# Last block of a three-layer model on one core: TensorE's order written by hand from the gates to the first out projection

## The chip, the core and the metric

The kernel runs on one core of a Trainium2 chip. A core has TensorE for matrix products (PE, with PEld for its weight loads), VectorE (DVE), ScalarE (ACT), GpSimd (POOL) and SyncE (SP), which here only starts transfers. The engines run beside each other, each through its own list of instructions in a fixed order, and wait for one another on semaphores. The metric is the time of one execution on the device in microseconds, the median over several runs.

## The reference, cut to what matters

Input is one sequence of 1024 tokens, 1024 wide, in 32-bit floats. Two layers of a first model come first (windowed attention beside a state-space mixer, then attention on selected keys). The change touches only the block behind them:

```
h    = layer_norm(x)
proj = h @ w_in                      # xs, z, bm, cm, dt, glu, cgate
xbc  = silu(causal_conv4(xs, bm, cm))
dt   = softplus(dt + dt_bias);  a_cs = cumsum(dt * a) in chunks of 128
y    = diagonal(cm, bm, a_cs, xs*dt) + off_diagonal(cm, state, a_cs) + d_skip*xs
y    = group_rms(y * silu(z)) * g
u    = glu[:1024] * sigmoid(glu[1024:])
u    = silu(layer_norm(causal_conv31(u))) * silu(cgate)
out  = concat(y, u) @ w_out + b_out
h    = layer_norm(ALPHA*h + out);  then a gated product and another layer norm
```

The scan over eight chunks carries a state per group (two groups of eight heads) from chunk to chunk. Both z and cgate ("the gates") are products of the normed input with parts of `w_in`.

## The kernel before, in words

All products are made in three passes of a split number: an operand is a rounded high part and the rest, and `mm3` (lines 149 to 151) adds high x high, high x low and low x high. A *product* here is one output tile of 128 x 512 over eight slices of 128 rows of the contraction: eight *steps* of three matmuls, 24 matmuls. The normed input lies transposed in one tile, `hnT`, for the whole block; weights are loaded in pieces of 128 x 512 by `wpiece` (SP starts the transfer, ScalarE or VectorE rounds, GpSimd or VectorE subtracts) into 13 rotating buffers, or into three more of the stage's own pool.

`phase_c` is the last block. In program order it makes: the GLU products, eight channel tiles of u; in `xbc` the products dt, bm, cm and xs with their short convolution (four taps, all on VectorE, lines 1544 and 1546); the long convolution of 31 taps on VectorE, one channel tile after the other, in two accumulation banks (1286 and 1288), and the sum over the channels in `acc` (1291); `conf_norm`, the layer norm over the channels: the mean by a matmul (1490), the subtraction on VectorE (1495), the squares on ScalarE (1497), their sum on GpSimd (1501), the variance by small matmuls (1505), its root on GpSimd, its spread over the rows by matmul (1510), the multiplication on VectorE (1515) and the silu on ScalarE (1516); `ssd`, first the step sizes (a softplus written out as a series, 1567 to 1611, whose running sums go to memory as `d_cs`), then the scan; the cgate products, 16 of them, stored to `d_cg`; the multiplication of the convolution's result by them (16 halves, GpSimd, 1313); the z products, 16 of them, stored to `d_z`; and the first half of the out projection (the lines from 1327 on), which reads the convolution's result split by ScalarE and GpSimd (`msC`, 1335 and 1336) and adds the residual and the bias.

In each chunk of the scan, per group: a tile of decays is loaded from `d_cs` (`ld`), shifted on VectorE (1629), made an exponential on ScalarE (1631) and multiplied by the product of cm and bm (1642); GpSimd scales the input to `xd`, `xe` and `xh` (1644 to 1647); TensorE makes `cb`, `yoff` from the state, `ydiag` from decay and `xd`, and `inc`, by which VectorE updates the state.

Who comes when is not the program's order. The framework orders each engine's instructions itself, by what it estimates to be ready, keeping what the data demand; only the marked `high_priority` and `issue_after` places push it. What it keeps is the order in which tiles of one tag take that tag's buffers: the program's order. TensorE has two banks for products (`mm`), three for the scan and the norm (`sd`), one for transposes and two for the long convolution. A pool that is closed hands its place to the next one, whose tiles wait until the old tile there is no longer read.

The block's second out projection follows, with its own layer norm, and then the gated product with the output.

Of the kernel before, what the change touches and what calls it, by code (L numbers as in the profile page):

```python
# [20 lines left out]
P = 128  # L21
L = 1024
# [35 lines left out]
class K:  # L58
# [94 lines left out]
    def form1(self, out, hnT, tok0, wt, nk, w, wc0=0, start=True, stop=True):  # L153

        for k in range(nk):
            self.mm3(out, hnT[:, 0, k, tok0:tok0 + P], hnT[:, 1, k, tok0:tok0 + P],
                     wt[k][:, 0, wc0:wc0 + w], wt[k][:, 1, wc0:wc0 + w],
                     start and k == 0, stop and k == nk - 1)

# [1078 lines left out]
def phase_c(k, out, hC):  # L1238
# [15 lines left out]
    def stage():  # L1254
        return stg.tile([P, 512], F32, tag="s", name="stg", bufs=3)
# [4 lines left out]
    sV, (up,) = stack(k.pool("c_u"))  # L1260
    for j in range(4):
# [14 lines left out]
    with ExitStack() as cx:  # L1276
        xbc(k, cx.enter_context(k.pool("c_xbc")), W, hnT, sw, dtt, d_xs, d_bc)

    acc = up.tile([P, L], F32, name="acc")
# [18 lines left out]
    for ch in range(2):  # L1298
        w = k.wchunk(W, 4624 + ch * 512, 512)
        for m in range(4):  # L1300
            for th in range(2):
                ps = k.mm()
                k.form2(ps, hnT, th * 512, w, KT, m * P)
                gt = stage()
                S.activation(gt, ps, AF.Silu)
                r0 = (ch * 4 + m) * P
                nc.scalar.dma_start(d_cg[r0:r0 + P, th * 512:th * 512 + 512], gt)
    for ct in range(8):
        for th in range(2):
            cs = slice(th * 512, th * 512 + 512)  # L1310
            cg = stg.tile([P, 512], F32, tag="cg", name="cgl", bufs=2)
            nc.sync.dma_start(cg, d_cg[ct * P:(ct + 1) * P, cs])
            G.tensor_tensor(cc[:, ct, cs], cc[:, ct, cs], cg, op=ALU.mult)
    for ch in range(2):
        w = k.wchunk(W, 1024 + ch * 512, 512)
        for tt in range(NT):
            ps = k.mm()
            k.form1(ps, hnT, tt * P, w, KT, 512)
            zt = stage()
            S.activation(zt, ps, AF.Silu)  # L1320
            nc.scalar.dma_start(d_z[tt * P:(tt + 1) * P, ch * 512:ch * 512 + 512], zt)
    sR.close()
    k.wdve = WDVE[4]

    with ExitStack() as co:
        op = co.enter_context(k.pool("c_o", side="right"))
        bo = op.tile([P, D], F32, name="bo")
        k.bcast_row(bo, ins["b_out_2"][0], D)
        w = [[k.wpiece(Wo, kk + 8, [(ch * 512, 512)], pool=op if ch * 8 + kk >= 13 else None, nx=3)
              for kk in range(8)] for ch in range(2)]  # L1330
        held = []
        for tt in range(NT):
# [6 lines left out]
            V.scalar_tensor_tensor(r, r, ALPHA, bo, op0=ALU.mult, op1=ALU.add)  # L1339
            held.append((tt, m, r))  # L1340
            if tt == NT - 2:
                continue
            for ch in range(2):
                cs = slice(ch * 512, ch * 512 + 512)
                for t_, m, r in held:
                    ps = k.mm()
                    k.form1(ps, m, 0, w[ch], 8, 512)
                    V.tensor_tensor(r[:, cs], ps, r[:, cs], op=ALU.add)
                    nc.sync.dma_start(d_r[t_ * P:(t_ + 1) * P, cs], r[:, cs])
            held = []  # L1350
    sS.close()
    sF.close()

# [4 lines left out]
    with ExitStack() as co:  # L1358
# [4 lines left out]
        k.bcast_row(bb, ins["ln1_b_2"][0], D)  # L1363
        w = [[k.wpiece(Wo, kk, [(ch * 512, 512)], scale=sng[:, kk:kk + 1], pool=op if ch * 8 + kk >= 13 else None, nx=3)
              for kk in range(8)] for ch in range(2)]

        def prep(tt):
# [19 lines left out]
            nc.sync.dma_start(r, d_r[ts_, :])  # L1387
            return m, r
# [19 lines left out]
        for tt in range(NT):  # L1408
            pt = op.tile([P, 256], F32, tag="pt", name="pt", bufs=2)
# [72 lines left out]
def conf_norm(k, p, cc, acc, cw):  # L1482
# [5 lines left out]
    for th in range(2):  # L1488
        ps = k.ps("sd", "mu")
        T.matmul(ps, on, acc[:, th * 512:th * 512 + 512], start=True, stop=True)  # L1490
        mu.append(ps)
    for ct in range(8):
# [11 lines left out]
    for tt in range(NT):  # L1504
        T.matmul(ps[:, tt * 2:tt * 2 + 2], acc[:, tt * P:(tt + 1) * P], on[:, 0:2], start=True, stop=True)
# [194 lines left out]
```

## Time and profile before

| | us |
|---|---|
| median of three timed runs (2117.3 to 2118.9) | 2117.71 |
| the profiled execution | 2112.16 |
| its span, first to last instruction | 2110.3 |
| TensorE busy (9291 matmuls) | 1931.6, 92% |
| VectorE busy | 1513.9, 72% |
| ScalarE busy | 845.0, 40% |
| GpSimd busy | 903.8, 43% |

A busy TensorE in this profile means that a matmul is in flight: matmuls are pipelined and overlap in the records. The granted clock tells at which share of full speed TensorE was let run. A releaser behind "<-" is what ended an engine's idle time. Times of rows are counted from the span's start; the block that changes runs from about 1150 to the end.

### The profile page before, as it was taken

The page shows a single profiled execution, that of the slowest core. Times are in us where ns is not written, and L with a number is a line of the kernel's source. Part 1 is how long each engine was busy: PE and PEld are TensorE (multiplying, and loading weights), DVE is VectorE, ACT ScalarE, POOL GpSimd, SP SyncE. Part 2 cuts the span into 40 slices and gives each one's busy share as a digit, 9 for nine tenths or more (in the row PEclk, how much of TensorE's full clock was granted, in tenths as well). Part 3 has the DMA queues.
Part 4 walks back from the last instruction along what each step waited for, and adds up shares of the span by engine and source line. Part 5 has one row for each costly group of instructions (what it writes and reads, how often), then busy time and mean ns, then how long its engine had stood idle before and what let it go on. Part 6 is the DMA issues. An engine that isn't in the chain of part 4 may idle for free. (4 is left out here: it accounts for less than half of the span.)

```text
span 2110.3 us, 27572 instructions
## 1 busy us (share of the span) xinstructions
PE 1931.6 (92%) x9291; PEld 1564.4 (74%) x9291; DVE 1513.9 (72%) x2995; ACT 845.0 (40%) x1604; POOL 903.8 (43%) x734
## 2 busy tenths in 40 slices
PE   7988889989999989799989899999999559999998
PEld 6767777777888878577867788788888447778786
DVE  8365513674469999788855399999997488857637
ACT  5223327564456896455546211223322411144210
POOL 5567416545322246365457221222232576643204
PEclk9989989999999999799999999999999879999999
DMA  6543332313222212643355222223433445475442
GB/s 199 151 125 102 115 129 83 120 44 110 81 61 71 70 51 87 198 169 121 116 159 185 85 89 71 75 80 100 127 113 99 161 139 171 160 247 172 166 153 100
DMA packets 166694, 256.19 MB, mean 121 GB/s; under 512 B 29078, under 2 KB 77548, under 8 KB 166554
## 3 DMA queue, kind: packets, MB, share of 16 engines
q1 hardware_dynamic: 154026, 232.43, 35.2%
q10 hardware_dynamic: 12528, 22.02, 2.8%
q8 instruction: 73, 1.20, 0.2%
q14 instruction: 67, 0.55, 0.1%
HBM read 185.35 MB, written 75.06 MB: 123 GB/s over the span
## 5 line engine op out<-in xcount | busy, mean ns | idle before, releaser
L124 POOL TENSOR_TENSOR w<-wraw,w 128x512 fp32r<-128x512 f32 (+1 forms) x230 | 311.9, 1371 | 665.9 <-ACT w L123 663.1
L1288 DVE SCALAR_TENSOR_TENSOR cy<-u,cw,cy 128x1024 f32<-128x1024 f32 x232 | 298.8, 1288 | 5.7
L123 ACT ACTIVATE w<-wraw 128x512 fp32r<-128x512 f32 (+1 forms) x230 | 140.9, 623 | 189.3 <-DMA wraw<-in_w_in_dram 55.1
L150 PE MATMUL mm<-hnTC,w 128*128 128x512 f32 (+1 forms) x336 | 131.6, 392 | 0.0
L151 PE MATMUL mm<-hnTC,w 128*128 128x512 f32 (+1 forms) x336 | 131.5, 391 | 0.0
L149 PE MATMUL mm<-hnTC,w 128*128 128x512 f32 (+1 forms) x336 | 131.5, 391 | 0.0
L1166 POOL TENSOR_TENSOR lgB<-lgB,sc 128x1024 f32<-128x1024 f32 (+5 forms) x48 | 84.5, 1791 | 77.4 <-DMA lgB<-d_T 69.3
L151 PE MATMUL mm<-w,ms 128*128 128x512 f32 x256 | 106.1, 415 | 10.1 <-POOL ms L1021 5.7
L149 PE MATMUL mm<-w,ms 128*128 128x512 f32 x256 | 105.0, 410 | 9.3 <-ACT ms L1020 9.2
L1077 ACT ACTIVATE tkj<-sc,tks 128x896 bf16<-128x896 f32 (+2 forms) x93 | 96.3, 1037 | 22.2 <-DVE tks L1073 16.4
L150 PE MATMUL mm<-w,ms 128*128 128x512 f32 x256 | 102.6, 401 | 0.3 <-POOL w L124 0.3
L169 POOL TENSOR_TENSOR hr<-hm,mhalf 128x2 f32<-128x2 f32 (+2 forms) x40 | 44.6, 1115 | 83.5 <-DVE hm L406 44.6
L149 PE MATMUL mm<-w,hnTA 128*128 128x512 f32 (+1 forms) x192 | 72.9, 383 | 7.7 <-DVE qo L409 7.7
L149 PE MATMUL mm<-w,hnTB 128*128 128x512 f32 x192 | 76.0, 397 | 3.2 <-ACT w L123 3.2
L149 PE MATMUL mm<-hnTB,w 128*128 128x512 f32 (+2 forms) x208 | 78.4, 377 | 0.4 <-DVE wit L868 0.4
L150 PE MATMUL mm<-hnTB,w 128*128 128x512 f32 (+2 forms) x208 | 78.1, 376 | 0.0
L151 PE MATMUL mm<-hnTB,w 128*128 128x512 f32 (+2 forms) x208 | 78.1, 375 | 0.0
L150 PE MATMUL mm<-w,hnTB 128*128 128x512 f32 x192 | 75.7, 394 | 2.0 <-POOL w L124 2.0
L151 PE MATMUL mm<-w,hnTB 128*128 128x512 f32 x192 | 75.4, 393 | 0.0
L151 PE MATMUL mm<-w,hnTA 128*128 128x512 f32 (+1 forms) x192 | 73.6, 384 | 0.0
L150 PE MATMUL mm<-w,hnTA 128*128 128x512 f32 (+1 forms) x192 | 73.0, 381 | 0.4 <-POOL w L124 0.4
L149 PEld LDWEIGHTS mm<-hnTC,w 128*128 128x128 f32 (+1 forms) x336 | 61.6, 183 | 14.5
(607 smaller groups left out, 5881.4 us busy)
## 6 DMA issues: line engine op xcount, KB each, us to landing
wraw<-in_w_in_dram SPq DMA_DIRECT2D x56, 256.0 KB
wraw<-in_od_w_in_dram SPq DMA_DIRECT2D x48, 256.0 KB
wraw<-in_ev_w_in_dram SPq DMA_DIRECT2D x32, 256.0 KB
wraw<-in_w_in_dram SPq DMA_DIRECT2D x64, 128.0 KB
wraw<-in_w_out_dram SPq DMA_DIRECT2D x32, 256.0 KB
ld<-d_cs SPq DMA_DIRECT2D x16, 512.0 KB
hr<-h SPq DMA_DIRECT2D x24, 256.0 KB
d_T<-d_row SPq DMA_DIRECT2D x8, 576.0 KB
```

The costliest lines, as they stand in the source:

```text
L123: nc.scalar.activation(t[:, 0, :o], raw[:, :o], AF.Copy)
L124: nc.gpsimd.tensor_tensor(t[:, 1, :o], raw[:, :o], t[:, 0, :o].bitcast(F32), op=ALU.subtract)
L149: mm(out, aH, bH, start=start, stop=False)
L150: mm(out, aH, bL, start=False, stop=False)
L151: self.last = mm(out, aL, bH, start=False, stop=stop)
L169: self.nc.gpsimd.tensor_tensor(out, ms, self.mhalf[:, :n], op=ALU.pow)
L1077: S.activation(self.junk(n), sc[b], AF.Sign, bias=cand[:, i:i + 1], accum_out=cnt[:, i:i + 1])
L1166: G.tensor_tensor(lg[:, :n], lg[:, :n], self.masks[b], op=ALU.add)
L1288: V.scalar_tensor_tensor(py if i < 30 else y, u[:, i:i + L], cw[:, ct, i:i + 1], py, op0=ALU.mult, op1=ALU.add)
```

## The change

TensorE's instructions from the cgate products to the end of the first out projection are put into one hand-written order. A generator, `filling`, runs through the cgate products, the z products and the out projection step by step (the new methods `steps1` and `steps2` are `form1` and `form2` that yield after each step); `take(n)` draws n steps. 128 + 8 steps come ahead of the channel mean (all cgate products, one z product), 30 behind it, 8 behind the variance, 20 behind its spread; then `ssd`, which now yields five times a chunk, has 4 or 3 steps drawn at each yield; the rest follows. Other engines' instructions are still ordered by the framework.

The step sizes are moved from the front of `ssd` into `xbc`, as `ssd_steps`, right behind the dt product, with their scratch in one of the two buffers of the tag `xy`. The first tap of the short convolution goes from VectorE to ScalarE. In the scan the scaled inputs are made in halves of 512, one a group, with two buffers (three for the loaded input), the decay tiles share one tag with three buffers where each group had one, and the last chunk's `xe` is left out. The gate tiles `cgl` share the tag `s`, now of four buffers, with the staging tiles of the products. The residual is scaled as the bank is added, and the bias is added on GpSimd in the second out projection. Weight pieces of the first out projection no longer go to VectorE in turn.

```diff
+    def steps1(self, out, hnT, tok0, wt, nk, w):
+        for k in range(nk):
+            self.mm3(out, hnT[:, 0, k, tok0:tok0 + P], hnT[:, 1, k, tok0:tok0 + P],
+                     wt[k][:, 0, :w], wt[k][:, 1, :w], k == 0, k == nk - 1)
+            yield
...
-    def stage():
-        return stg.tile([P, 512], F32, tag="s", name="stg", bufs=3)
+    def stage(name="stg"):
+        return stg.tile([P, 512], F32, tag="s", name=name, bufs=4)
...
-    conf_norm(k, up, cc, acc, cw)
-    sV.close()
-    sS, (sp,) = stack(k.pool("ssd"))
-    ssd(k, sp, dtt, dtx, d_xs, d_bc, d_ys, d_cs)
...
-            cg = stg.tile([P, 512], F32, tag="cg", name="cgl", bufs=2)
...
+        for ch in range(2):
+            w = k.wchunk(W, 1024 + ch * 512, 512)
+            for tt in range(NT):
                 ps = k.mm()
+                yield from k.steps1(ps, hnT, tt * P, w, KT, 512)
+                zt = stage()
+                S.activation(zt, ps, AF.Silu)
+                nc.scalar.dma_start(d_z[tt * P:(tt + 1) * P, ch * 512:ch * 512 + 512], zt)
+        sR.close()
+        op = held.enter_context(k.pool("c_o", side="right"))
...
-            V.scalar_tensor_tensor(r, r, ALPHA, bo, op0=ALU.mult, op1=ALU.add)
...
+                    yield from k.steps1(ps, m, 0, w[ch], 8, 512)
+                    V.scalar_tensor_tensor(r[:, cs], r[:, cs], ALPHA, ps, op0=ALU.mult, op1=ALU.add)
...
+    with tc.manual_schedule(engines={mybir.EngineType.PE}):
+        take(128 + 8)
+        norm = conf_norm(k, up, cc, acc, cw)
+        for n in (30, 8, 0):
+            next(norm)
+            take(n)
+        next(norm, None)
+        for ct in range(8):
+            for th in range(2):
+                cs = slice(th * 512, th * 512 + 512)
+                cg = stage("cgl")
+                nc.sync.dma_start(cg, d_cg[ct * P:(ct + 1) * P, cs])
+                G.tensor_tensor(cc[:, ct, cs], cc[:, ct, cs], cg, op=ALU.mult)
+        sV.close()
+        sS, (sp,) = stack(k.pool("ssd"))
+        take(20)
+        for i, _ in enumerate(ssd(k, sp, steps, dtt, dtx, d_xs, d_bc, d_ys, d_cs)):
+            take(4 - i % 2)
+        take(500)
...
+            G.tensor_tensor(r, r, bo, op=ALU.add)
...
-            V.tensor_scalar(y, xi[:, 0:L], sw[:, ct, 0:1], sw[:, ct, 4:5], op0=ALU.mult, op1=ALU.add)
+            S.activation(y, xi[:, 0:L], AF.Identity, scale=sw[:, ct, 0:1], bias=sw[:, ct, 4:5])
...
+    t8 = p.tile([P, 8, P], F32, tag="xy", name="spt", bufs=2)
...
-            ld = p.tile([P, 8, P], F32, tag=f"ld{g}", name="ld", bufs=1)
+            ld = p.tile([P, 8, P], F32, tag="ld", name="ld", bufs=3)
...
+        yield
+        xds, xes = [], []
+        for g in range(2):
+            xd = p.tile([P, 512], F32, tag="xd", name="xd", bufs=2)
...
```

## Rows read from the trace of the kernel before

**Rows 1.** The page: span, and busy tenths in 40 equal slices of the span.
```profile
span 2110.3 us, 27572 instructions
...
DVE  8365513674469999788855399999997488857637
ACT  5223327564456896455546211223322411144210
```

**Rows 2.** Busy time by stretch: length, PE, PEld, DVE, ACT, POOL, granted clock, DMA.
```profile
1667.00:1701.00 34.00, 0.00 (x0) 0.00 (x0) 33.05 (x57) 15.32 (x16) 18.75 (x14) 0.54 0.71 242
...
1715.00:1859.00 144.00, 133.26 (x647) 101.97 (x647) 118.99 (x110) 25.21 (x29) 100.76 (x47) 0.95 0.49 153
...
1881.00:2004.00 123.00, 120.40 (x591) 97.98 (x589) 88.95 (x150) 48.90 (x96) 38.00 (x28) 1.00 0.53 179
```

**Rows 3.** TensorE in order of time: start, length, instruction, count, idle before.
```profile
1623.02 1.45 PE L1490 MATMUL mu<-acc,ones 128*128 128x512 f32 x3
...
1656.74 1.84 PE L1505 MATMUL var<-ones,acc 128*128 128x2 f32 x16
...
1701.03 0.77 PE L1598 MATMUL acs<-spt,tri 128*128 128x128 f32 x2 [34.40 <-DVE spt L1587]
...
1715.07 3.65 PE L1656 MATMUL ydiag<-xd,ld 128*128 128x64 f32 x16 [10.05 <-DVE ld L1642]
...
1721.64 1.89 PE L1656 MATMUL ydiag<-xd,ld 128*128 128x64 f32 x16
...
1881.36 0.38 PE L182 MATMUL tph<-ident,yO 128*128 128x128 f32 x2
```

**Rows 4.** VectorE in order of time: last channel sum, first subtraction, a step-size piece.
```profile
1609.89 1.23 DVE L1291 TENSOR_TENSOR acc<-acc,cc 128x1024 f32<-128x1024 f32 x1
...
1624.30 1.28 DVE L1495 TENSOR_TENSOR cc<-cc,mu 128x512 f32<-128x512 f32 x2
...
1692.25 0.29 DVE L1574 TENSOR_TENSOR spt<-spt 128x128 f32<-128x128 f32 x1
```

**Rows 5.** Line 1544: shortest/median/longest ns, first and last start; waits ahead.
```profile
L1544 DVE TENSOR_SCALAR xy<-xi,sw x12: 779/809/1398, 1360.4 to 1486.0; 128x1024 f32<-128x1024 f32 x12
...
  ACT xi L1542: 2.9, 5
```

**Rows 6.** ScalarE in order of time: z eviction, first square, table load, silu.
```profile
1590.57 0.60 ACT L1320 ACTIVATE stg<-mm 128x512 f32<-128x512 f32 x1 [4.84 <-PE mm L151]
...
1629.80 1.06 ACT L1497 ACTIVATE sqc<-cc 128x1024 f32<-128x1024 f32 x1 [4.64 <-DVE cc L1495]
...
1674.80 1.28 ACT L1516 ACT_TABLE_LOAD   x1
1676.09 2.37 ACT L1516 ACTIVATE cc<-cc,cw 128x1024 f32<-128x1024 f32 x2
```

**Rows 7.** GpSimd in order of time: the last sum of squares.
```profile
1649.00 2.40 POOL L1501 TENSOR_TENSOR acc<-acc,sqc 128x1024 f32<-128x1024 f32 x1 [0.55 <-ACT sqc L1497]
```

**Rows 8.** Groups by line from 1350 on: busy us, mean ns, idle before.
```profile
L1336 POOL TENSOR_TENSOR msC<-cc,msC 128x1024 fp32r<-128x1024 f32 x8 | 22.3, 2796 | 16.1 <-ACT msC L1335 16.1
...
L1515 DVE TENSOR_TENSOR cc<-cc,rb 128x512 f32<-128x512 f32 x16 | 9.6, 677 | 0.0
```

**Rows 9.** Line 1313, the gate multiplication: shortest/median/longest ns.
```profile
L1313 POOL TENSOR_TENSOR cc<-cc,cgl x16: 1255/1272/2247, 1677.4 to 1719.1; 128x512 f32<-128x512 f32 x16
```

**Rows 10.** TensorE in order of time in the scan: chunk starts and one wait.
```profile
1743.88 0.38 PE L1634 MATMUL cb<-bct 128*128 128x128 f32 x2
...
1757.44 2.07 PE L1663 MATMUL inc<-xe,bt 128*128 128x512 f32 x2 [3.06 <-POOL xe L1646]
...
1768.09 0.38 PE L1634 MATMUL cb<-bct 128*128 128x128 f32 x2
...
1785.66 0.38 PE L1634 MATMUL cb<-bct 128*128 128x128 f32 x2
...
1803.24 0.38 PE L1634 MATMUL cb<-bct 128*128 128x128 f32 x2
```

More of the change, by code (lines that the diff above doesn't have):

```diff
@@ L158, in form1, with steps2 @@
                      start and k == 0, stop and k == nk - 1)
+    def steps1(self, out, hnT, tok0, wt, nk, w):
[3 more added lines that the diff above has]
+            yield
+    def steps2(self, out, hnT, tok0, wt, nk, m0):
+        for k in range(nk):
+            self.mm3(out, wt[k][:, 0, m0:m0 + P], wt[k][:, 1, m0:m0 + P],
+                     hnT[:, 0, k, tok0:tok0 + 512], hnT[:, 1, k, tok0:tok0 + 512], k == 0, k == nk - 1)
+            yield
     def form2(self, out, hnT, tok0, wt, nk, m0, m=P):
@@ L1260, in phase_c @@
     sV, (up,) = stack(k.pool("c_u"))
+    acc = up.tile([P, L], F32, name="acc")
     for j in range(4):
@@ L1322, in phase_c, with filling @@
[L1322 to L1328, printed above, removed]
+    held = ExitStack()
+    def filling():
+        for ch in range(2):
+            w = k.wchunk(W, 4624 + ch * 512, 512)
+            for m in range(4):
+                for th in range(2):
+                    ps = k.mm()
+                    yield from k.steps2(ps, hnT, th * 512, w, KT, m * P)
+                    gt = stage()
+                    S.activation(gt, ps, AF.Silu)
+                    r0 = (ch * 4 + m) * P
+                    nc.scalar.dma_start(d_cg[r0:r0 + P, th * 512:th * 512 + 512], gt)
+        for ch in range(2):
+            w = k.wchunk(W, 1024 + ch * 512, 512)
+            for tt in range(NT):
+                ps = k.mm()
+                yield from k.steps1(ps, hnT, tt * P, w, KT, 512)
[4 more added lines that the diff above has]
+        op = held.enter_context(k.pool("c_o", side="right"))
@@ L1408, in phase_c @@
         for tt in range(NT):
-            pt = op.tile([P, 256], F32, tag="pt", name="pt", bufs=2)
+            pt = op.tile([P, D], F32, tag="z", name="pt", bufs=2)[:, :256]
             nc.sync.dma_start(pt, ins["p_2"][0, 0][tt * P:(tt + 1) * P, :])
@@ L1491, in conf_norm @@
         mu.append(ps)
+    yield
     for ct in range(8):
@@ L1526, in xbc @@
         k.form2(ps[:16], hnT, th * 512, w, KT, 0, 16)
-        dr = p.tile([16, 512], F32, tag="dr", name="dr", bufs=1)
+        dr = p.tile([P, 512], F32, tag="xo", name="dr", bufs=2)[:16]
         S.activation(dr, ps[:16], AF.Copy)
@@ L1563, in ssd @@
     f = lambda a: a.rearrange("p a b -> p (a b)")
-    t = p.tile([P, 4, P], F32, tag="ld0", name="spt", bufs=1)
+    t8 = p.tile([P, 8, P], F32, tag="xy", name="spt", bufs=2)
+    t = t8[:, 0:4]
     a3 = lambda i: t[:, i].rearrange("p (a b) -> p a b", b=16)
```

104 lines of the change are left out of this document (53 added, 51 removed).

## The prediction

> **What bounds the kernel now.** I read the page first [rows 1]: 2110.3 us of span inside a profiled execution of 2112.16 us, so 1.9 us lie around the span; the three timed runs have a median of 2117.71, 5.55 us above the profiled one. The sums below are made in the profiled time, and 5.55 is added at the end. Then the busy time by stretch [rows 2]. TensorE does nothing from 1667 to 1701, at a granted clock of 0.54, almost all of it the 1.2 GHz level; in the scan, 1715 to 1859, it is busy 133 of 144 us; in the stage behind it, 1881 to 2004, 120 of 123. So the changed stretch has one large hole, and what comes behind it starts when TensorE is through with the first out projection: its first transpose for the second one stands at 1881.36 [rows 3]. The question is at what time that row stands afterwards.
>
> TensorE's own order of time [rows 3] shows what made the hole. The channel mean runs at 1623.02, the variance at 1656.74; then, with the gate products used up, TensorE stands 34.40 us until the step sizes are ready, and 10.05 us more for the decay tile. VectorE [rows 4] shows why the mean came when it did: the last channel sum ends at 1609.89 + 1.23 = 1611.1, so the mean ran 11.9 us late, because its place in TensorE's order was behind nine z products.
>
> **The change part by part.** *Up to the mean.* Twelve first taps of the short convolution leave VectorE for ScalarE: 12 x 0.81 = 9.7 us, and with the 2.9 us that VectorE waited ahead of five of them 12.6 [rows 5]. ScalarE gets 12 activations, by the nearest row 2.37 / 2 = 1.2 us each [rows 6], 14 us in slices (the 26th to 29th of 52.8 us) that are two to three tenths busy [rows 1]: nothing. Into the same stretch come the 33 VectorE instructions of the step sizes, out of the hole; alone, a piece takes 0.29 us [rows 4], 9.6 in all. They are a chain of their own among two others, so part of it falls into the others' gaps: 0 to 9.6, I take 5.7, nearer the row. VectorE is nine tenths busy or more in each slice from the 24th to the 30th [rows 1], so the last channel sum moves by -9.7 + 5.7 = -4 (bounds -12.6 to 0) to 1607.1. Their exponentials, the triangle on GpSimd and the store of the running sums lie under work that does not set this time; the step sizes hold one of the two buffers of the convolved tile meanwhile, which can only make TensorE later than it need be, and it has room:
>
> *The wait that this adds.* Each z product takes 0.60 + 4.84 = 5.44 us [rows 6], a step of eight 0.68. With one z product instead of nine ahead of the mean, TensorE is there 8 x 5.44 = 43.5 us earlier, at 1579.5, and about 1 us later for the three small matmuls of the step sizes, so at 1580.5. It then stands 27 us for VectorE, and every other product is queued behind. So the hole at 1667 does not vanish; part of it comes up here.
>
> *Mean to scan.* The mean runs at 1607.3; VectorE's subtractions began 1.28 us after it [rows 3, 4], so 1608.6; from there to the last sum of squares on GpSimd were 1649.00 + 2.40 - 1624.30 = 27.1 us [rows 4, 7], so 1635.7. The 30 steps laid over it are 20.4 us, after 1.3 to 2.6 for the mean. A restart costs: after the 10 us hole the diagonal took 3.65 us, the next one 1.89 [rows 3], half pace from 1715.07 to 1721.6; I take 3 us for each restart. So TensorE is at the variance at 1633.3 and waits until 1635.9. Variance 1.7, eight steps 5.4 (over them the root, an instruction on one column a tile, is hidden), the spread over the rows, again 16 small matmuls, 1.7: 1644.7. VectorE multiplies, 16 in 9.6 us [rows 8], 0.60 each. In the subtractions, which have the same shape, ScalarE's first square came 5.5 us in, that is after the ninth instruction, not the second [rows 4, 6]; I take the same (lower bound 1.8): 1650.4. The silu takes 1.2: 1651.7.
>
> *The staging tiles.* The gate values coming back used two buffers of their own; now they share four with what TensorE's z products put out, and a tag's buffers are handed out in program order. The sixth z product's staging tile comes behind all sixteen gate tiles and so needs the thirteenth freed. TensorE has two banks for products: it runs the two steps left of the sixth and the seventh, 10 steps, 6.8 us, until 1651.5, and then stands until GpSimd has multiplied thirteen halves. These take 1.27 (median) [rows 9], 16.5 us, and more where loads are late; I take 17.5: 1669.2, evicted at 1670.1. That is a stand of 18.6 us. Then the other 10 steps with a restart, 9.8: the scan begins at 1679.9; before, its first diagonal stood at 1715.07.
>
> *Scan.* Forty yields take 4 or 3 steps, 140 in all: 95.2 us. A chunk without waits ran from 1785.66 to 1803.24 [rows 10], two products (10.9) in it, so 6.7 of its own, eight times less one last update 52.7. Together 147.9, or 18.5 a chunk. Waits: before, TensorE was idle 144 - 133.3 = 10.7 us in the scan [rows 2]. Now one of three decay tiles can be loaded ahead where each group had one, and VectorE loses the pass over the residual; bounds 0 and 10.7, I take 4. In chunk three the gates end and the out projection begins: its split tile lies where TensorE's last z operand lay, so after the last z matmul come an eviction 0.60 and a copy 1.06 [rows 6], the subtraction 2.80 on GpSimd [rows 8] with up to one more instruction ahead of it there, and a restart: 8 (bounds 4.5 and 20, where the out projection's eleven late weight pieces, those for which none of the 13 buffers is free while the gates still use eight, stand ahead with 1.4 each, half of that subtraction). End: 1679.9 + 147.9 + 12 = 1839.8.
>
> *After it.* Of 256 steps 8 + 30 + 8 + 20 + 140 are gone; 50 are left, 34.0 us, more than the 22 us (1859 to 1881.36) over which the second projection's first tiles were prepared before, so no new gap: 1873.8 instead of 1881.36, 7.6 us earlier. The bias addition moves to GpSimd's stage behind, eight passes by 2.8, as [rows 8] for a tile of that size, under a TensorE that is 98% busy there: 0, and at most 5 if GpSimd delays a tile. The second load of each chunk's input adds eight issues to SP, the bias row and the token tiles of the last inputs only change place: 0. Weight pieces that VectorE took now go to ScalarE and GpSimd; that stands in the 20 above.
>
> Sum: 2112.2 - 7.6 = 2104.6 in the profile, about 2110 as a median of timed runs. With the bounds of its own terms (-12.6 or 0, 1.8 for 5.5, 16.5 to 20, waits 0 to 10.7, 4.5 to 20), not all at one end, this case reaches from 2100 to 2121.
>
> **Rivals.** *No hold (0.18).* If the sixth z product does not wait for the gate multiplications, because its buffer comes free sooner, the 18.6 us and the restart go: 2088. For it: GpSimd is free from 1639 on, and the gates wait for it alone. Against: the order of the buffers in the program.
>
> *GpSimd paces the scan (0.17), slower.* In the chunk from 1743.88 to 1768.09 TensorE waited for the two scaled inputs, 3.06 us for the second [rows 10], and the chunk took 24.2 us. TensorE could still slide products then; now it stands at the place written. If the four chunks around the change from gates to out projection, where the weight pieces fall on GpSimd, cost that, it is 4 x (24.2 - 18.5) less the 2 counted, 21 us: 2131. It decides once GpSimd's work in a chunk passes 18.5 us; it was busy 100.8 of 144 us in the scan [rows 2], 70%, and buffers of half the size let it begin sooner, which speaks against.
>
> *The hole only moves (0.15).* VectorE gains nothing before the mean (+4), and the change from gates to projection costs 12: 2118, no change. For it: the mean still waits for VectorE, the scan for GpSimd, and TensorE's filler is the same.
>
> *Table loads (0.05).* ScalarE loads its table anew between silu and exp: 1.28 us each, and the next activation starts right behind it [rows 6]. Now eight silus fall between eight exponentials in the first four chunks, up to 16 loads, 20.5 us: if the exponentials were on the path, 2130. ScalarE was busy 25.2 of 144 us in the scan [rows 2], so I hold that they hide.
> The Trainium skill, page "ScalarE: Activation LUTs", section "What ACT_TABLE_LOAD costs", gives 1283 ns for the load and another 1380 for the drain, about 2.66 us a switch, and the section "Table sets: the hidden batching unit" wants activations batched by set, which this change undoes. The trace agrees with the load and shows no drain behind it. By the page's figure the rival would be an estimated 42 us, 2152.
>
> **How the numbers follow.** The forecast has 0.45. Less than 0.2%, 4.2 us, cannot be told from no change: the borders are 2113.5 and 2121.9. Of the forecast's range two thirds lie below, a quarter within. Faster: 0.30 + 0.18 + 0.01 = 0.49; within: 0.11 + 0.12 = 0.23; slower: 0.04 + 0.17 + 0.05 + 0.02 = 0.28. Range 2087 to 2132: it takes in the no-hold case, the forecast, the unchanged one and most of GpSimd's pace.
>
> **What would show it.** Right, if the mean follows the last channel sum within 1 us, with TensorE idle 20 to 30 us ahead of it at the low clock; if TensorE is idle 10 to 20 us behind the spread with GpSimd's gate multiplication or the eviction named; if the scan's chunks take 18.5 to 19.5 us; and if the first transpose of the second projection stands near 1874. Wrong, if the channel sum ends outside 1598 to 1613, if the gates pass without a stand behind the spread, or if chunks take over 21 us.

## The result and the profile after

The changed kernel takes 2135.36 us (median of 4 runs, 2133.86 to 2140.58), the kernel before beside it 2118.31 (2117.30 to 2119.46): a ratio of 1.0088, 95% interval 1.0076 to 1.0101. It is 17 us slower, where 8 us faster was forecast, and above the range.

The page after: span, busy times, and TensorE's line in tenths, 40 slices of the span.
```profile
span 2134.3 us, 27655 instructions
...
PE 1936.4 (91%) x9291; PEld 1567.1 (73%) x9291; DVE 1465.0 (69%) x2959; ACT 879.1 (41%) x1637; POOL 922.6 (43%) x772
...
PE   7988899999999989799988899999985698999998
...
```
The hole from 1667 to 1701 [rows 2] became shallower and longer: the 31st and 32nd slice, 53 us each, are five and six tenths busy, and the empty time in them is split up.

Where the time went is read best by stretches, each worked out from the first start of a tile on TensorE in the trace. "Start" runs from the block's first product to the first step-size product, "region" from there to the first transpose of the second projection (the stretch of the forecast), "stage" from that to the last gate product. All kernels of this study stand here, so that the experiments can refer to it; each has one profiled execution. Kernels that do not differ in a stretch agree there within some 2 us in start and region (552.4 to 554.0 in after, e1, e4 and e10), but only within 5 us in the stage (220.6 to 225.5 in the nine with the late bias), so a single stage proves little.
```
kernel            block at   start  region  stage | timed median, ratio to before (95%)
before              1145.7   190.7   544.9  218.7 | 2118.3
after               1153.2   195.0   553.4  222.4 | 2135.4  1.0088 (1.0076 to 1.0101)
e1_acc_late         1148.7   196.2   552.4  225.5 | 2134.4  1.0076 (1.0061 to 1.0090)
e2_cg_own           1150.4   195.3   538.4  222.7 | 2121.2  1.0011 (1.0001 to 1.0022)
e3_ahead48          1150.1   194.9   552.1  223.6 | 2133.7  1.0075 (1.0056 to 1.0095)
e4_no_bias          1152.7   195.0   553.3  219.1 | 2130.1  1.0053 (1.0036 to 1.0069)
e5_accr             1153.7   192.4   540.2  220.6 | 2117.4  0.9991 (0.9977 to 1.0004)
e6_ahead24          1149.2   191.4   529.7  225.1 | 2102.2  0.9913 (0.9892 to 0.9934)
e7_pause            1157.0   192.1   543.6  223.2 | 2122.0  1.0012 (0.9998 to 1.0027)
e8_biasv            1147.1   191.5   538.9  224.1 | 2118.2  0.9998 (0.9984 to 1.0012)
e9_auto             1152.7   195.6   542.4  223.4 | 2126.1  1.0032 (1.0018 to 1.0047)
e10_biasearly       1151.3   195.0   554.0  218.9 | 2132.4  1.0070 (1.0050 to 1.0090)
e11 (24, early)     1152.9   191.1   527.5  220.5 | 2103.0  0.9927 (0.9909 to 0.9945)
e12 (32, early)     1148.9   192.3   534.4  219.3 | 2107.8  0.9955 (0.9938 to 0.9971)
```
From before to after: start +4.3, region +8.5, stage +3.7, together 16.5 of the 17 us timed. That the block begins 7.5 us later (1153.2 against 1145.7) is no part of it: the engines' instructions ahead of it stand in the same order in both programs, the other kernels begin it anywhere from 1147 to 1157, and the profiled execution of before lies 6 us under its own median.

In the region TensorE's work did not change, its stands did; a stand is time in which it is idle. (TensorE alone, before, then after: length, busy time and matmuls, granted clock, DMA share, GB/s.)
```profile
1336.47:1881.36 544.89, 489.78 (x2254) 0.95 0.42 133
1348.17:1901.61 553.44, 490.18 (x2255) 0.94 0.40 130
```
It stands 55.1 us before and 63.3 after, which is 8.2 of the 8.5 us. In every other kernel but e7 it is busy 490 to 493 us of its region too, so the regions differ by their stands.

TensorE after, in order of time (start, length, instruction, count, idle before and what ended it). To compare with before, take off 11.70 us: the first step-size product stands at 1348.17 and stood at 1336.47.
```profile
1619.80 3.78 PE L1522 MATMUL mu<-acc,ones 128*128 128x512 f32 x4 [27.99 <-DVE acc L1305]
...
1649.58 3.48 PE L1538 MATMUL var<-ones,acc 128*128 128x2 f32 x16 [4.47 <-POOL acc L1534]
...
1660.17 1.95 PE L1544 MATMUL rb<-ident,rsc 128*128 128x128 f32 x16
...
1688.37 0.79 PE L149 MATMUL mm<-w,hnTC 128*128 128x512 f32 x1 [19.42 <-ACT stg L1327]
...
1697.98 0.38 PE L1682 MATMUL cb<-bct 128*128 128x128 f32 x2
...
1717.97 0.27 PE L1682 MATMUL cb<-bct 128*128 128x128 f32 x1
...
1757.26 0.38 PE L1682 MATMUL cb<-bct 128*128 128x128 f32 x2
...
1759.98 1.02 PE L1707 MATMUL yoff<-st,bct 128*128 128x512 f32 x2
1760.44 0.79 PE L149 MATMUL mm<-w,hnTC 128*128 128x512 f32 x1
1761.07 0.40 PE L150 MATMUL mm<-w,hnTC 128*128 128x512 f32 x1
1761.30 0.39 PE L151 MATMUL mm<-w,hnTC 128*128 128x512 f32 x1
...
1772.03 0.50 PE L149 MATMUL mm<-w,msC 128*128 128x512 f32 x1 [4.28 <-ACT msC L1337]
...
1779.13 0.79 PE L151 MATMUL mm<-w,msC 128*128 128x512 f32 x1 [6.33 <-POOL msC L1338]
...
1789.59 0.38 PE L1682 MATMUL cb<-bct 128*128 128x128 f32 x2
...
1901.61 0.60 PE L196 MATMUL tph<-ident,yO 128*128 128x128 f32 x4
1904.91 0.63 PE L196 MATMUL tph<-ident,yO 128*128 128x128 f32 x4 [2.70 <-DVE smS L1410]
```
These rows answer to [rows 3, 10]. Every stand that was forecast is there: 27.99 us ahead of the mean, 19.42 us for the staging tile, the change from gates to projection.

Busy time after by stretch (length, then PE, PEld, DVE, ACT, POOL, granted clock, DMA share, GB/s).
```profile
1592.00:1619.70 27.70, 0.00 (x0) 0.00 (x0) 26.97 (x21) 1.30 (x3) 2.54 (x2) 0.56 0.14 41
1645.20:1649.50 4.30, 0.00 (x0) 0.00 (x0) 0.00 (x0) 0.57 (x1) 4.22 (x2) 1.00 0.10 37
1649.60:1653.00 3.40, 3.40 (x17) 3.40 (x17) 0.00 (x0) 0.00 (x0) 0.00 (x0) 0.52 0.00 0
1653.00:1656.50 3.50, 3.50 (x10) 2.73 (x10) 0.17 (x1) 0.60 (x1) 1.66 (x1) 0.50 0.00 0
1656.50:1662.20 5.70, 5.70 (x35) 5.01 (x34) 0.87 (x2) 0.00 (x0) 0.00 (x0) 1.00 0.51 176
...
1697.98:1717.97 19.99, 19.99 (x102) 15.89 (x100) 11.47 (x12) 7.10 (x10) 12.82 (x12) 1.00 0.59 196
...
1757.26:1789.59 32.33, 21.72 (x98) 16.16 (x97) 10.98 (x13) 14.41 (x20) 25.59 (x19) 0.84 0.59 206
```
TensorE is busy 19.99 of the first chunk's 19.99 us, so outside the chunk in which the gates end the scan is TensorE's own now ([rows 2] had 133 of 144): the other engines can't be blamed for the length of such a chunk. The chunks take 19.99, 19.31, 19.99, 32.33, 20.02, 19.31 and 21.01 us from start to start, by four or three steps at a yield 18 or 17 steps each.

### The profile page after: what moved, and what is told of

Same layout as the page of the kernel before. It is cut to its first block, busy times and chain, and to the rows that moved or that the text cites. A ratio compares the mean times of both kernels' runs of the same rounds, so it can differ in the third digit from the quotient of the medians.

```text
span 2134.3 us, 27655 instructions
## 1 busy us (share of the span) xinstructions
PE 1936.4 (91%) x9291; PEld 1567.1 (73%) x9291; DVE 1465.0 (69%) x2959; ACT 879.1 (41%) x1637; POOL 922.6 (43%) x772
## 4 chain that ended last, share of the span: by engine, by line
PE 47%; DVE 22%; DMA 10%; issue 9%; POOL 6%; ACT 4%; SPq 2%; DVEq 0%; POOLq 0%; ACTq 0%
PE mm L151 8%; PE mm L149 8%; PE mm L150 8%; DVE cy L1302 6%; DVE tkj L1093 2%; POOL w L124 2%; PE pb L149 1%; PE pb L150 1%; PE pb L151 1%; PE pg L149 1%; PE pg L150 1%; PE pa L149 1%; PE pg L151 1%; PE pa L150 1%; PE pa L151 1%
## 5 line engine op out<-in xcount | busy, mean ns | idle before, releaser
L124 POOL TENSOR_TENSOR w<-wraw,w 128x512 fp32r<-128x512 f32 (+1 forms) x238 | 324.1, 1377 | 633.1 <-ACT w L123 632.4
L123 ACT ACTIVATE w<-wraw 128x512 fp32r<-128x512 f32 (+1 forms) x238 | 145.3, 622 | 188.8 <-DMA wraw<-in_w_in_dram 50.1
L1180 POOL TENSOR_TENSOR lgB<-lgB,sc 128x1024 f32<-128x1024 f32 (+5 forms) x48 | 84.5, 1788 | 79.2 <-DMA lgB<-d_T 58.0
L149 PE MATMUL mm<-w,hnTC 128*128 128x512 f32 x128 | 59.4, 464 | 19.4 <-ACT stg L1327 19.4
```

Source lines behind the costliest of these rows:

```text
L123: nc.scalar.activation(t[:, 0, :o], raw[:, :o], AF.Copy)
L124: nc.gpsimd.tensor_tensor(t[:, 1, :o], raw[:, :o], t[:, 0, :o].bitcast(F32), op=ALU.subtract)
L149: mm(out, aH, bH, start=start, stop=False)
L1180: G.tensor_tensor(lg[:, :n], lg[:, :n], self.masks[b], op=ALU.add)
```

## The experiments

The theories at the start: the loss is the sum of three parts, a late load at the block's start, stands fixed by the written order in the region, and the late bias in the stage. The rival: only the region counts, and the rest is one execution's chance.

**e1: the channel sums' tile taken late.**
```
-    acc = up.tile([P, L], F32, name="acc")      # head of the block
...
+    acc = up.tile([P, L], F32, name="acc")      # behind the short convolution
```


> The changed kernel with one line moved back: the tile of the channel sums is taken from its pool after the short convolution again, not at the head of the last block. Theory: that tile, taken first, put the buffers for the parameter rows of the last block into another place, where stores of the block before still read; the first transpose of those rows moved from 1164.32 to 1179.75 us and waited 8.71 us for its load, and 4.3 us of that stayed to the end. Expected: that transpose within 13 us of the first projection product of the block and a median of about 2131 us, 4 below the changed kernel's 2135.4. Rival: the late rows are one execution's chance or lie beside other work; then the time stays at 2135 (2133.5 to 2137).


2134.4 us, and the rows as late as in the changed kernel (their first transpose 28.3 us after the block's start, in the changed kernel 26.6, in the kernel before 18.6): a miss, which leaves open what late rows cost. The parameter rows are issued behind the last store of the preceding block all the same.

**e2: gate values in buffers of their own.**
```
-        return stg.tile([P, 512], F32, tag="s", name=name, bufs=4)
+        return stg.tile([P, 512], F32, tag="s", name=name, bufs=2)
...
-                cg = stage("cgl")
+                cg = stg.tile([P, 512], F32, tag="cg", name="cgl", bufs=2)
```


> The changed kernel, but the gate values that come back use two buffers of their own again and the staging ring has two tiles instead of four. Theory: the 19.4 us in which TensorE stands behind the spread over the rows is the sixth z product's staging tile, handed out behind the sixteen gate tiles; with buffers of their own it goes, TensorE runs its 20 steps at once and is at the scan 19 us earlier, but there the first diagonal needs the scaled input from GpSimd, whose sixteen gate multiplications (1.27 us each) come before it in its order, until about 1691 on this trace's clock. So part of the hole comes up again: I expect a stand of 6 to 10 us at the first diagonal and a median of 2121 to 2127 us. Rival 1 (the ring is the whole price): all 19.4 us and the restart go, 2113 to 2116. Rival 2 (GpSimd's gate multiplications set the scan's start anyway): 2134 to 2136.


2121.2 us, 14 less; the region 15.0 us shorter. TensorE around the scan's start:
```profile
1673.21 0.38 PE L1682 MATMUL cb<-bct 128*128 128x128 f32 x2
...
1681.11 0.54 PE L150 MATMUL mm<-w,hnTC 128*128 128x512 f32 x1 [2.48 <-POOL w L124]
...
1755.26 0.79 PE L149 MATMUL mm<-w,msC 128*128 128x512 f32 x1 [5.95 <-ACT msC L1337]
...
1762.21 0.80 PE L151 MATMUL mm<-w,msC 128*128 128x512 f32 x1 [5.73 <-POOL msC L1338]
```
The 19.4 us stand is gone, 2.5 us of it came back for a weight piece that GpSimd made late, not at the diagonal, and the stand at the end of the gates stayed. So the ring was the cause of that stand, and it was worth 14 us, not the 22 of the "no hold" rival: the scan began 22.3 us earlier after the region's start, and 7 of these were lost again behind it.

**e3: 40 steps ahead of the mean instead of 8.**
```
-        take(128 + 8)
+        take(128 + 40)
```


> The changed kernel with 40 instead of 8 steps of z products (five products instead of one) ahead of the channel mean; all else as it was. Theory: the 28.0 us in which TensorE stands for VectorE ahead of the mean is empty time, 32 more steps (21.8 us) fill it without moving the mean, and as many fewer are left behind the scan. The z products then end, and the out projection begins, about two chunks of the scan earlier, at a cost of some us if its weights or its split tile are late. Expected: stand ahead of the mean 5 to 8 us, mean within 1 us of where it was against the start of the block, median 2113 to 2117. Rival (what sets the end is not TensorE's work but the chain of VectorE, ScalarE and GpSimd behind the channel mean): 2133 to 2137, with the stand reappearing in the scan.


2133.7 us, nothing gained: the rival's number, but not its cause. TensorE:
```profile
1616.65 3.78 PE L1522 MATMUL mu<-acc,ones 128*128 128x512 f32 x4 [6.27 <-DVE acc L1305]
1656.05 3.57 PE L1538 MATMUL var<-ones,acc 128*128 128x2 f32 x16 [14.21 <-POOL acc L1534]
...
1897.06 1.97 PE L196 MATMUL tph<-ident,yO 128*128 128x128 f32 x8 [11.02 <-ACT yO L1414]
```
and GpSimd ahead of that variance:
```profile
1635.74 2.41 POOL L1534 TENSOR_TENSOR acc<-acc,sqc 128x1024 f32<-128x1024 f32 x1
1638.09 2.56 POOL L124 TENSOR_TENSOR w<-wraw,w 128x512 fp32r<-128x512 f32 x2
1640.60 2.40 POOL L1534 TENSOR_TENSOR acc<-acc,sqc 128x1024 f32<-128x1024 f32 x1
1642.92 2.52 POOL L124 TENSOR_TENSOR w<-wraw,w 128x512 fp32r<-128x512 f32 x2
```
The stand ahead of the mean went from 28.0 to 6.3 us as expected, but weight pieces of the out projection fell between the sums of squares and the variance came 9.6 us later behind the mean. The first half of the z weights was used up early, their buffers came free, and the next weights were loaded at once (eight pieces of `w_out`, issued from 1635.82 on). The staging hold stayed (20.18 us). Behind the scan the filling then ran out: 11 us of waiting for the second projection's first tile.

**e4: no output bias.**
```
-            G.tensor_tensor(r, r, bo, op=ALU.add)
```


> The changed kernel without the output bias of the last block: neither its row is loaded nor is it added (GpSimd's eight additions ahead of the second out projection go). Theory: the addition sits on GpSimd among the split operands that TensorE waits for, and makes 3 to 4 us of the 18: the second projection's stage from its first transpose to the end takes 229 us as before the change instead of 232.7, median 2131 to 2132. Rival (the addition hides under TensorE, as I predicted, and the 3.8 us is the clock or chance): 2134 to 2137, and the stage keeps 232 us.


This kernel leaves out the bias. 2130.1 us, 5 less; the stage takes 219.1 us, near the 218.7 of the kernel before. Its first transposes lose the 2.70 us wait of after:
```profile
1901.00 0.60 PE L196 MATMUL tph<-ident,yO 128*128 128x128 f32 x4
1902.03 0.63 PE L196 MATMUL tph<-ident,yO 128*128 128x128 f32 x4 [0.43 <-DVE rC L1349]
```

**e5: on e2's ring, the channel sums on the other side of memory, their dead halves as gate buffers.**
```
-    acc = up.tile([P, L], F32, name="acc")
+    acc = sR.enter_context(k.pool("c_acc", side="right")).tile([P, L], F32, name="acc")
...
-                cg = stage("cgl")
+                cg = acc[:, cs]
```


> As the run in which the gate values had two buffers of their own and the staging ring two tiles (2121.2 us), with one more edit: the tile of the channel sums lies in a pool of its own on the other side of memory, and its two halves, dead after the variance, are the two gate buffers. So the pool of the convolution buffers starts 4096 bytes higher, at byte 182784 and no longer at 178688, above the pool of the block before, which ends at 181024. Theory: what made the parameter rows late was that this pool reached down into the one of the block before (the step-size tiles, kept longer now, push it down by 2624 bytes), not the order in which the tile of the channel sums was taken (moving that alone gave 2134.4). Expected: the first transpose of the rows within 5 us of where it stood in the kernel before, the 4.3 us gone, 2116 to 2118. Rival (those 4.3 us are covered later): 2120 to 2122 with the rows early all the same.


2117.4 us, 3.8 below e2, with the start 2.9 us shorter (192.4; over all six kernels with this edit 191.8 on average, over the seven others with the change 195.3). SyncE's issues before, after, and in e5 (start, length, store or load):
```profile
1152.16 0.29 SPq L1458 DMA_DIRECT2D rows<-in_conf_conv_w_dram  x1
```
```profile
1161.51 8.43 SPq L111 DMA_DIRECT2D wraw<-in_w_in_dram  x8
1170.36 0.33 SPq L1016 DMA_DIRECT2D d_h<-hr  x1
1170.73 0.29 SPq L1490 DMA_DIRECT2D rows<-in_conf_conv_w_dram  x1
```
```profile
1161.09 0.33 SPq L1016 DMA_DIRECT2D d_h<-hr  x1
1161.46 0.29 SPq L1490 DMA_DIRECT2D rows<-in_conf_conv_w_dram  x1
...
1165.21 0.38 SPq L1046 DMA_DIRECT2D h<-hr  x1
```
In e5 the rows go out ahead of the weights and of the last stores, 7.8 us after the block's start, where the kernel before had 6.5 and the changed one 17.5. So it was the place of the pool, as far as moving it shows: tiles that live longer at one end of a memory stack had pushed a pool into the one of the preceding block.

**e6: 24 steps ahead of the mean, on e5.**
```
-        take(128 + 8)
+        take(128 + 24)
```


> As the run sent ahead of it in this set (channel sums on the other side, gate values in their halves), with 24 instead of 8 steps of z products ahead of the channel mean. Theory: 40 steps ahead failed (2133.7) not because the stand ahead of the mean is worthless but because the z weights of the first half were used up 16 steps earlier than the variance, so that weight pieces of the out projection fell on GpSimd between the sums of squares (eight pieces of 1.3 us) and the variance came 10 us late, and the staging hold behind it stayed. With 24 steps the half is used up only behind the spread over the rows: the stand ahead of the mean goes from 28 to 17 us, the variance stays, and the end comes 8 to 11 us earlier, 2106 to 2110 if the run ahead of it gives 2117. Rival (the chain of VectorE, ScalarE and GpSimd behind the mean sets the end, whatever TensorE has done): no gain, within 2 us of the run ahead of it.


2102.2 us, ratio 0.9913 (0.9892 to 0.9934) to the kernel before: faster than both kernels. The region is 10.5 us shorter than in e5, inside the 8 to 11 expected; timed it is 15 less, with an uncertainty of some 5, and below the 2106 to 2110 expected. TensorE:
```profile
1612.43 3.41 PE L1522 MATMUL mu<-acc,ones 128*128 128x512 f32 x4 [17.39 <-DVE acc L1305]
...
1640.74 3.57 PE L1538 MATMUL var<-ones,acc 128*128 128x2 f32 x16 [4.46 <-POOL acc L1534]
```
The wait for the variance did not grow. Two z products more in an empty stretch are time won, as long as their weights don't free buffers too early.

**e7: a pause in the filling at the end of the gates, on e5.**
```
+            if tt == 0:
+                yield
...
-            take(4 - i % 2)
+            take(0 if 18 <= i < 23 else 4 - i % 2)
```


> As the first run of this set, but when the last z step is issued the out projection is only prepared (its split tile, its weights), and five pauses of the scan take no filling step; the out projection's products begin behind them and the steps left out run behind the scan. Theory: the 12 us that TensorE stands between the last z product and the first of the out projection (6.0 for ScalarE's copy, 5.7 for GpSimd's subtraction) lie in TensorE's written order alone; the scan's own work, 7.75 us a chunk, can run in them. Expected: that stand falls to 5 us or less and the end comes 5 to 9 us earlier than in the first run of this set. Rival (the scan without filling waits for VectorE and GpSimd as long as TensorE stood, a chunk of 18 us or more): within 2 us of it.


2122.0 us, 4.7 slower than e5, where the intervals touch. The rival was right in its cause, and the time is above its 2 us:
```profile
1761.45 0.79 PE L1684 MATMUL cb<-bct 128*128 128x128 f32 x2 [4.84 <-DVE yS L1711]
...
1765.60 3.65 PE L1715 MATMUL ydiag<-xd,ld 128*128 128x64 f32 x16 [0.63 <-DVE ld L1692]
...
1772.24 2.05 PE L1709 MATMUL yoff<-st,bct 128*128 128x512 f32 x2 [1.19 <-DVE yS L1711]
...
1782.03 2.07 PE L1722 MATMUL inc<-xe,bt 128*128 128x512 f32 x2 [2.20 <-POOL xe L1701]
```
Without filling the scan waits for VectorE and GpSimd, 8.9 us in four places in place of 10.3 in two (4.53 and 5.77 in e5), and much of it at the lower clock (0.59 granted from 1759 to 1788; the first diagonal takes 3.65 us, the second 1.91).

**e8: the late bias on VectorE, on e5.**
```
-            G.tensor_tensor(r, r, bo, op=ALU.add)
+            V.tensor_tensor(r, r, bo, op=ALU.add)
```


> As the first run of this set, with the eight additions of the output bias on VectorE instead of GpSimd. Leaving them out gave 2130.1 against 2135.4, so on GpSimd they cost 5 us although GpSimd is not the engine that is full in that stage. Theory: the price is the place, between the gated product and the root that the same tile's scaling waits for on GpSimd; on VectorE it goes, 2 to 5 us below the first run. Rival: VectorE, which evicts both projections' products there, delays them by as much (1.2 us a tile): within 2 us, or slower.


2118.2 us, the same as e5: the rival. On VectorE the bias costs no less than on GpSimd.

**e9: no written order.**
```
-    with tc.manual_schedule(engines={mybir.EngineType.PE}):
+    with ExitStack():
```


> The changed kernel without the order written by hand: the framework's planner orders TensorE's work again from the gates to the first out projection, while the early step sizes, the shared staging ring, the halved buffers of the scan and the late bias stay. It tells how much of the loss is the written order itself. Theory: the written order fixes where TensorE stands (28.0 us ahead of the mean, 19.4 us for the ring, 10.6 at the end of the gates), but a planner that counts no such stand has about as much empty time elsewhere; with the early rows late (4.3), the bias on GpSimd (5) and the ring as before I expect 2125 to 2138, the mean later than in the changed kernel and the empty time behind it. Rival 1 (the written order is what cost the time): 2112 to 2119. Rival 2 (it saved time against what the other edits cost): above 2140.


2126.1 us, 9 below the changed kernel, at the lower end of what was expected; the region is 11.0 us shorter, and start and stage are within 1 us of the changed kernel's. TensorE:
```profile
1624.39 1.88 PE L1522 MATMUL mu<-acc,ones 128*128 128x512 f32 x4
1650.13 3.57 PE L1538 MATMUL var<-ones,acc 128*128 128x2 f32 x16 [23.86 <-POOL acc L1534]
```
The planner ran seven z products (56 steps) up to the mean, which so came 4.5 us later and without a stand, and left 24 us behind it empty. In the region TensorE stands 50.6 us, 12.7 less than in the changed kernel; with the same shared ring only 1.5 us of them are for a staging tile, so the ring is dear only in the written order. The written order with its counts cost the region 11 us against it, and the other edits saved the region 2.5 us against the kernel before (542.4 against 544.9); which of them did so was not taken apart.

**e10: the bias early again.**
```
+            V.scalar_tensor_tensor(r, r, ALPHA, bo, op0=ALU.mult, op1=ALU.add)
...
-            G.tensor_tensor(r, r, bo, op=ALU.add)
```


> The changed kernel with the output bias where it was before the change: its row is loaded for the first out projection and added on VectorE with the scaled residual there, and the second projection has no addition. All else as in the changed kernel. Theory: late, the bias costs 5 us on whichever engine (without it 2130.1 against 2135.4; on VectorE 2118.2 against 2117.4 on GpSimd), because it delays tiles that the layer norm and TensorE behind it wait for; in the scan VectorE has the time for eight passes of 1.2 us. Expected 2129.5 to 2131.5, and the stage behind the first transpose of the second projection as long as in the kernel before. Rival (VectorE's pass, 1.2 us a tile, comes between the scan's own steps and delays TensorE in the written order): 2133 to 2137.


2132.4 us, 3 less than the changed kernel and 1 above the range given; the intervals overlap. The stage is 218.9 us, as predicted, the region 554.0 against 553.4. Over all traces the stage is 223.4 us on average in the nine kernels with the late bias and 219.5 in the four without it or with the early one: 3.9 us, in time 5 (e4), 3 within the uncertainty (e10), and none where e11 is held against e6.

**e11 and e12: e5 with the early bias of e10, and with 24 and 32 steps ahead.**
```
-        take(128 + 8)
+        take(128 + 24)      # e12: 128 + 32
```


> As the run with 24 steps ahead of the mean, the channel sums on the other side and the gate values in their halves (2102.2 us), with the output bias added early, in the first out projection, as before the change. Theory: the same 3 to 5 us as without these edits: 2097 to 2100. Rival: in this order the end is set by the tail of the second projection's preparation, where the bias now stands, or VectorE's pass delays the scan: 2101 to 2104.


2103.0 us. The stage is 4.6 us shorter than in e6, but the median isn't: which of the two is better isn't settled.

> As the run before it, with 32 instead of 24 steps ahead of the mean. Theory: one more product (5.4 us) out of the 17 us stand ahead of the mean, while the z weights of the first half are used up between the mean and the variance, at its 24th step there, so the first weight pieces of the out projection can meet the last sums of squares on GpSimd. Expected: 2 to 5 us below the run before it if no piece falls there before the variance, 2093 to 2098. Rival: the variance comes several us later, as with 40 steps ahead, where it came 10 us late, and nothing is gained: 2099 to 2106.


2107.8 us, 4.8 slower than e11 (the intervals just overlap): the rival. The variance of e12:
```profile
1648.03 3.57 PE L1538 MATMUL var<-ones,acc 128*128 128x2 f32 x16 [10.50 <-POOL acc L1534]
```
The wait that e6 had at 4.46 us is 10.50, with weight pieces on GpSimd again between the sums of squares. The gain ends where the filling reaches the last product on the first half of the z weights, its steps 57 to 64, ahead of the variance: 54 steps are drawn there in e6, 62 in e12 and 70 in e3, and six pieces of `w_out` are issued in e12 then, eight in e3.

## Why the prediction was wrong

On the forecast's clock the first transpose of the second projection stands at 1901.61 - 11.70 = 1889.9, not at 1873.8: 16.1 us of error in the region, 4.3 ahead of it and 3.7 behind it make 24 of the 25 us between forecast and result.

Of the signs that were named, the first two held: the mean followed the last channel sum at once, behind a stand of 27.99 us at a granted clock of 0.56, and 19.42 us stood behind the spread with the eviction named. The chunks (18.5 to 19.5 us) and the transpose (1874) did not come true: most chunks took 20 us, and two passed the 21 us that were named as a sign of being wrong.

**Up to the mean** the sum was right: TensorE at the mean at 1619.80 - 27.99 - 11.70 = 1580.1 (1580.5), the mean at 1608.1 (1607.3). VectorE reached the last channel sum 3.1 us earlier, where 4 were taken; how much of that the first taps and the step sizes make, each by itself, no run shows.

**Restarts** were the first mis-sized term. A restart was priced at the mean and behind the long stands, and none at the variance, where TensorE stood only 4.47 us. The granted clock was 1.00 in that stand and 0.50 to 0.52, the 1.2 GHz level, for the 6.9 us of work behind it: the variance took 3.48 us instead of 1.7 and the eight steps behind it 7.1 instead of 5.4. So the spread began at 1648.5, not at 1643.0 (1644.7 less its own 1.7): 2.0 us of that had come with the variance (1637.9 for 1635.9), 3.5 are the low clock.

**The staging hold** was right in its mechanism and size: 19.42 us for 18.6, shown by e2. It ended at 1676.7 for 1670.1 and the scan began at 1686.3 for 1679.9, 6.4 late: 5.5 from the spread, and 1.4 because the thirteen gate multiplications took 18.9 us (1668.79 to 1687.69) where 17.5 were taken; the other steps came out 0.5 shorter. Three of the thirteen took 2.25 us each, beside VectorE's decay shifts (1671.98 to 1678.01), the others 1.26 to 1.28.

**"Two products (10.9) in it, so 6.7 of its own"** is the step that failed most. A chunk of 18 steps takes 19.99 us with TensorE busy throughout, so its own work is 19.99 - 18 x 0.68 = 7.75 us; eight chunks make 7.5 us more than forecast (8 x 1.05, less 0.9 because two updates are left out in the last chunk where one was counted). The chunk of the kernel before that was priced, 1785.66 to 1803.24, did not hold two products, which are 48 matmuls. Its matmuls of the filling (length, busy time and count of these alone, granted clock, DMA share, GB/s):
```profile
1785.66:1803.24 17.58, 11.28 (x43) 1.00 0.57 181
```
They are 43, that is 14 1/3 steps or 9.75 us, and leave 17.58 - 9.75 = 7.8 us for the chunk itself, the same as after the change. So the chunk did not become dearer; its filling had been counted too high. That is not seen by adding up records, because they overlap: at 1759.98 the state product (yoff, plain float32) has two records that end 1.02 us later, yet the next matmul's record starts after 0.46 us. From 1759.98 to 1761.07, where the matmul behind that one starts, are 1.09 us, and 0.23 is what a matmul of the filling takes from its start to the next one's, so 0.86 are the state product's.
The Trainium skill, page "FP8 and Floating Point Precision", section "TensorE Precision Notes", says that true FP32 takes four passes through the array. Four times the 0.23 us of such a matmul would be 0.92 us, an estimate; the trace's 0.86 agrees with it.

**Gates to projection** cost 32.33 us less a chunk of 17 steps, 19.31, so 13.0 instead of 8, within its bounds: 4.28 us for ScalarE's copy, 6.33 for GpSimd's subtraction, the rest the low clock. ScalarE rounded two weight pieces ahead of the eviction, and GpSimd had a scan addition, two scaled inputs and a weight piece ahead of its subtraction, where one instruction at most had been counted. Other waits in the scan made about 1 us where 4 were taken. Arrival 6.4, own work 7.5, this 5.0, waits -2.9 are 16.0 of the 16.1 us.

**The step sizes' place in memory** had no term; their work was priced on the engines alone ("under work that does not set this time"). Their tiles, 2624 bytes that now live to the end of the scan, moved a pool of another purpose into the preceding block's, and the first row load went out 17.5 us after the block's start instead of 6.5: 4.3 us at the start, of which 3.5 go with the pool's place (e5 and its followers) and 0.8 stay open. e1 shows that it isn't the order alone in which the tile of the channel sums was taken. Nothing in the profile of before shows it: the sizes of the pools do.

**"0, and at most 5 if GpSimd delays a tile"**: it was 3.7 us in the trace, near the bound. TensorE is busy 215.7 us of the stage in after as in e10, and stands 6.8 us against 3.1: 2.70 for the second group of transposes and 1.45 for the layer norm's tile 113 us into the stage, two waits that e4 and e10 lack. GpSimd is busy 81 of the stage's 222 us, so it was not the engine's load; on VectorE the price is no smaller (e8).

The rivals: GpSimd did not pace the scan (12.82 of 19.99 us busy in the first chunk) but in the one chunk in which the gates end, where it is busy 25.59 of 32.33 us and TensorE waits 6.33 for it. "The hole only moves" was right in its second half, the change from gates to projection (13.0 us where it says 12), and wrong in its first, since the channel sum came 3.1 us earlier. With that and the eight z products taken away from ahead of it the mean came 14.9 us earlier after the region's start than before (271.6 against 286.5 us), and none of it reached the end. Table loads did not show: ScalarE loads its tables thirteen times, six times ahead of z evictions and seven ahead of exponentials, and no chunk waited for an exponential.
The Trainium skill's 1283 ns for a load (page "ScalarE: Activation LUTs", section "What ACT_TABLE_LOAD costs") agrees with the 1283 ns of all thirteen; of its drain the trace shows nothing again: the first exponential starts at 1677.30, its load ended at 1676.01 + 1.28 = 1677.29.

So the sum of causes: the written order +11.0 in the region against the planner's, the other edits there -2.5, the late rows +4.3, the late bias +3.7: 16.5 of 17 us timed. The order's part is shown by e9. Of the late rows' 4.3 us e5 shows 3.5, and the bias is shown in the traces by e4 and e10, in the time by e4 alone. How the order's 11 us split into the ring and the other stands is not shown: e2 takes the ring away, but moves what comes behind too.

## What to carry to other kernels

A written order pays where its counts match the stands: fill the empty stretch ahead of a late input first, but stop before the filling frees buffers whose next loads land on the engine that this input comes from. Before sharing buffers or keeping tiles longer, look at what is handed out between them in program order, and at which neighbour's memory the stack grows into. Count the matmuls of a stretch before dividing its time; where records overlap, price an instruction from its start to that of the one after its successor, less what the successor takes.

## What was not expected of the hardware

Even a stand of 2.48 us was followed by the lower clock. Busy time in e2, columns as above, in that stand and behind it:
```profile
1678.60:1681.10 2.50, 0.03 (x1) 0.00 (x0) 2.50 (x3) 2.47 (x3) 2.50 (x3) 1.00 0.61 198
1681.10:1684.00 2.90, 2.89 (x10) 2.48 (x10) 1.98 (x2) 2.89 (x6) 1.65 (x1) 0.56 0.62 174
```
The clock was 1.00 in the stand and 0.56 in the work behind it, as it was 1.00 and then 0.50 to 0.52 around the 4.47 us stand of the changed kernel. The 4.47 us stand cost 3.5 us more in what followed it. A stand of 2.34 us in e5 was followed by 1.00 (1728.70 to 1731.00).
